# Turning the output gates of four memory heads together and ahead of the softmax, in a two-layer encoder on one core

## The chip, the core and the metric

The kernel runs on one core of a Trainium2 chip. That core has five engines, each with its own instruction stream that is worked off in order: TensorE (PE: matmuls, with PEld for the loading of their stationary operand), VectorE (DVE), ScalarE (ACT), GpSimd (POOL) and SyncE (SP), which here does almost nothing but start DMA transfers. The transfers themselves run on 16 DMA engines. The metric is the device time of one execution in microseconds (us); a clock of 1.00 in the tables is TensorE at full speed.

## The reference

Input: 256 tokens of 2048 numbers, float32, and 256 memory tokens. Two layers, each of this form:

```python
h = rmsnorm(x, norm_g[l]);  proj = h @ w_in[l]
a_x, a_b, a_c, a_g, d_q, d_k, d_v, d_g, m_q, m_g = split(proj)
y_a = short_gated_conv(a_x, a_b, a_c, ...) * silu(a_g)          # 6 groups of 128 columns
y_d = rmsnorm(diff_attention(q, k, v, ...)) * (1 - lam) * silu(d_g)   # 6 heads of 128
mk, mv = from the memory tokens and w_mem_kv[l]
mq = rmsnorm(m_q per head)
y_m = (softmax(mq @ mk.T * 128 ** -0.5) @ mv) * silu(m_g)       # 4 heads of 128
x = x + concat(y_a, y_d, y_m) @ w_out[l]
```

The change concerns the line of `y_m`: `softmax(...)` is a 256x256 matrix for each of four heads, and `silu(m_g)` holds, for each head, 256 tokens by 128 columns.

## The kernel before

**The main stream.** All weights come from HBM in loads of two k-tiles (`load_w`, L289, on SP's queue: 512 KB as one DMA, or two of 256 KB, four buffers). ACT rounds a load to `hi` (L292), DVE computes `lo`, the raw weights less `hi` (L293), and PE multiplies both with the split activations (L303: 12 matmuls of 128x512 for each load, three products for each of two token tiles and two k-tiles). `hi` and `lo` have four buffers too. In the text, weight loads are counted over the whole program in the order in which SP starts them. A projection block of 512 columns takes eight loads.

**The side work.** Between the blocks' matmuls stand pieces of attention, written as Python generators. A task is put into a list with a due number of chunks (`later`), and at each chunk of the stream the due generators run on to their next `yield`. So a `yield 4` sets how many chunks later the next step stands in the instruction streams. Counters `held` keep the tasks within the buffers: two softmax tiles `e`, two sheets `sh`, two tiles `yn`. Pins (`keep_in_program_order`) and a scheduler set the final order on each engine.

**Turning a matrix.** The attention needs matrices with rows and columns exchanged. DVE transposes blocks of 32x32 within a tile, and `carry` (L423 to L434) exchanges the blocks by way of DRAM: four DMAs write the sheet out (L430), two chunks later four read it back (L434). All eight are on SP's queue, where the weight loads stand too, and a read waits on SP for the landing of the writes.

**A memory pair** (`mem_pair`, two of the four heads; two pairs for each layer). `mem_scores` splits the turned queries `mqT` into two parts (ACT L604, L606; DVE L605, L607), multiplies with the keys (PE L613 to L615, tile `s`), takes exponentials `e` and gives back `e` and `r`, the reciprocal of the row sums times the half token scale `st[:, HR]`. The pair then transposes `e` into a sheet `sh`, multiplies the gate rows `mga` of each head by `r` into `yn` (L651, two for each head), transposes `yn` (L654), and carries first `sh` and then `yn` through DRAM. Last, PE computes `po` (L686): values times turned softmax weights, with channels on the partitions, and DVE multiplies `po` by the turned `yn` into the final `y`. A pair holds one of the two `yn` buffers, which the differential heads' pairs (`pair`) use as well, from before its transposes to its end.

The gate rows `mga` come from the projection block of `m_g`: `silu2` (L436 to L441) writes them, one 128x512 half for each token tile.

Of the kernel before, what the change touches and what calls it, by code (L numbers as in the profile page):

```python
# [10 lines left out]
F32 = mybir.dt.float32  # L11
# [3 lines left out]
ALU = mybir.AluOpType  # L15
# [3 lines left out]
P = 128  # L19
D_MODEL = 2048  # L20
SEQ = 256
DEPTH = 2
NT = SEQ // P
KT = D_MODEL // P
W_MEM = 512
# [3 lines left out]
DH = W_DIFF // P  # L29
# [3 lines left out]
NB = 512  # L33
# [3 lines left out]
B = 32  # L37
NA = P // B
# [10 lines left out]
def encoder(ctx: ExitStack, tc: tile.TileContext, x, mem, norm_g, w_in, conv_w, conv_b,  # L49
            dq_g, dk_g, lq1, lk1, lq2, lk2, head_g, mem_norm_g, w_mem_kv, mq_g, mk_g, w_out, out):  # L50
    nc = tc.nc
# [9 lines left out]
    keep = pool("keep", 1)  # L61
    tmp = pool("tmp", 2)
# [8 lines left out]
    def nm(s):  # L71
        uid[0] += 1
        return f"{s}_{uid[0]}"
# [134 lines left out]
    side, tasks = deque(), []  # L208
# [3 lines left out]
    def later(g, n):  # L212
        due[id(g)] = chunk[0] + n
        return g
# [181 lines left out]
    def sheet(home, tag, n=NB // P):  # L396
        return home.tile([P, NA, n, NT, B], F32, tag=tag, name=nm("sh"))
# [27 lines left out]
    def carry(sheet, to):  # L425


        d = dram.tile([NA, B, NA, sheet.shape[-1]], F32, name=nm("d"))
        for a in range(NA):
            tc.keep_in_program_order(nc.sync.dma_start(d[:, :, a].rearrange("b c r -> c b r"), sheet[a * B:(a + 1) * B]))  # L430
        yield 2
        of = d.rearrange("b c a (n i) -> (b c) a n i", i=B)
        for a in range(NA):
            tc.keep_in_program_order(nc.sync.dma_start(to[:, :, a], of[:, a]))  # L434

    def silu2(dst, src, st, t):  # L436

        n = src.shape[-1]
        th = tmp.tile([P, NB], F32, tag="nat", name=nm("th"), bufs=3)
        nc.scalar.activation(th[:, 0:n], src, AF.Tanh, scale=col(st, HR, t))  # L440
        nc.vector.scalar_tensor_tensor(dst, th[:, 0:n], 1.0, src, ALU.add, ALU.mult)  # L441

    def strips(v):
        return v.rearrange("p (b c) -> p b c", c=B)
# [63 lines left out]
    held = {"e": 0, "sh": 0, "yn": 0}  # L508
# [89 lines left out]
    def mem_scores(l, h, st):  # L598
        while l not in queries:
            yield 1  # L600
        qT, parts = queries[l]
        q, k, g = qT[:, h], mkT[l][:, h], mgain[:, l:l + 1]
        qh, ql, kh, kl = (parts[:, j] for j in (2 * (h % 2), 2 * (h % 2) + 1, 4, 5))
        pin(nc.scalar.copy(qh, q))  # L604
        pin(nc.vector.tensor_tensor(ql, q, qh.bitcast(F32), ALU.subtract))  # L605
        pin(nc.scalar.activation(kh, k, AF.Copy, scale=g))  # L606
        pin(nc.vector.scalar_tensor_tensor(kl, k, g, kh.bitcast(F32), ALU.mult, ALU.subtract))  # L607
        yield 1
        sc = P ** -0.5
        s = ps_s.tile([P, NT, SEQ], F32, tag="s", name=nm("s"))  # L610
        for i in range(NT):
            at = slice(i * P, (i + 1) * P)
            nc.tensor.matmul(s[:, i, :], qh[:, at], kh, start=True, stop=False)  # L613
            nc.tensor.matmul(s[:, i, :], qh[:, at], kl, start=False, stop=False)
            nc.tensor.matmul(s[:, i, :], ql[:, at], kh, start=False, stop=True)  # L615
        mx = small.tile([P, NT], F32, tag="mmx", name=nm("mmx"))
        nc.vector.tensor_reduce(mx, s, AX.X, ALU.max)
        nc.vector.tensor_scalar(mx, mx, -sc, None, ALU.mult)
        sm = small.tile([P, NT], F32, tag="msm", name=nm("msm"))
        e = tmp.tile([P, NT, SEQ], F32, tag="e", name=nm("me"))  # L620
        for i in range(NT):
            nc.scalar.activation(e[:, i], s[:, i], AF.Exp, bias=mx[:, i:i + 1], scale=sc, accum_out=sm[:, i:i + 1])
        r = small.tile([P, NT], F32, tag="mr", name=nm("mr"), bufs=6)
        nc.vector.reciprocal(r, sm)
        nc.vector.tensor_tensor(r, r, st[:, HR], ALU.mult)
        return e, r

    spare, yTs = {}, {}

    def mem_pair(l, n, a, st):  # L630
        heads = (2 * n, 2 * n + 1)
        es = []
        for h in heads:
            while held["e"] == 2:
                yield 1
            held["e"] += 1
            es.append((yield from mem_scores(l, h, st)))
            yield 2
        yield 4
        while held["sh"] == 2 or held["yn"] == 2:  # L640
            yield 1
        held["sh"] += 1
        held["yn"] += 1
        sh = tmp.tile([P, NA, 2, NT * NT, B], F32, tag="sh", name=nm("sh"))
        yn = tmp.tile([P, NA, 2, NT, B], F32, tag="yn", name=nm("yn"))
        for i, (e, r) in enumerate(es):
            tc.keep_in_program_order(nc.vector.transpose(
                sh[:, :, i], e.rearrange("p t (k b c) -> p b (t k) c", k=NT, b=NA)))
            held["e"] -= 1
            for t in range(NT):  # L650
                nc.vector.tensor_scalar(yn[:, :, i, t], strips(a[:, t, heads[i] * P:(heads[i] + 1) * P]),  # L651
                                        r[:, t:t + 1], None, ALU.mult)
            yield 1
        tc.keep_in_program_order(nc.vector.transpose(yn, yn))  # L654
        yield 4
        eT = sh.rearrange("p b h n c -> p (b h n c)")
        yT_ = yn.rearrange("p b h t c -> p (b h t c)")
        yield from carry(sh.rearrange("p b h n c -> p b (h n c)"), eT.rearrange("p (n a i) -> p n a i", a=NA, i=B))
        yield from carry(yn.rearrange("p b h t c -> p b (h t c)"), yT_.rearrange("p (n a i) -> p n a i", a=NA, i=B))
        if n == 0:  # L660
            spare[l] = [keep.tile([P, 3, NB], F32R, tag=tag, name=nm(tag)) for tag in ("v", "ga")]
        hi, lo = spare[l]

        def split(j, src):
            tc.keep_in_program_order(nc.scalar.copy(hi[:, j], src))
            tc.keep_in_program_order(nc.vector.tensor_tensor(lo[:, j], src, hi[:, j].bitcast(F32), ALU.subtract))

        yield 1
        for k in range(NT):
            c = slice(k * SEQ, (k + 1) * SEQ)  # L670
            src = mv[l][:, k, n * SEQ:(n + 1) * SEQ]
            tc.keep_in_program_order(nc.scalar.copy(hi[:, 0, c], src))
            tc.keep_in_program_order(nc.vector.tensor_tensor(lo[:, 0, c], src, hi[:, 0, c].bitcast(F32), ALU.subtract))
        split(1, eT[:, 0:NB])
        yield 1
        split(2, eT[:, NB:2 * NB])
        held["sh"] -= 1
        yield 1
        for i, h in enumerate(heads):
            po = ps_t.tile([P, SEQ], F32, tag="t", name=nm("po"))  # L680
            at = 0
            for k in range(NT):
                vh, vl = (t[:, 0, k * SEQ + i * P:k * SEQ + (i + 1) * P] for t in (hi, lo))
                eh, el = (t[:, 1 + i].rearrange("p (t k q) -> p t k q", t=NT, k=NT)[:, :, k] for t in (hi, lo))
                for left, right in ((vh, eh), (vh, el), (vl, eh)):
                    nc.tensor.matmul(po, left, right, start=at == 0, stop=at == 3 * NT - 1)  # L686
                    at += 1
            y = yT_[:, i * SEQ:(i + 1) * SEQ]
            nc.vector.tensor_tensor(y, po, y, ALU.mult)
            yield 2  # L690
            assert all((l, d) in scored for d in range(DH))
            split_T(yTs[l], CG + DH + h, y, None, pin=True)
        held["yn"] -= 1

    def rows_T(src, k, n):

# [272 lines left out]
    while s < DEPTH * KT:  # L969
        l, k = divmod(s, KT)  # L970
# [24 lines left out]
    for l in range(DEPTH):  # L995
        st = stats_of(ssx, "st")
# [12 lines left out]
        def begin_pair(n, p):  # L1009
            tasks.append(later(p, max(1, start + PAIR_EVERY * n - chunk[0])))  # L1010
# [4 lines left out]
        for b in order:  # L1015
            if b in begun:
                acc = x_block([(C_D + b * NB, NB)], ALLK[-QT:], acc=begun[b])
            else:
                acc = x_block([(C_D + b * NB, NB)], ready=m.ready if l == 0 and b == order[0] else None)
# [21 lines left out]
                        silu2(ga[:, t, 256:768], acc[t], st, t)  # L1041

        mqT = keep.tile([P, MH, SEQ], F32, tag="mqT", name=nm("mqT"))
        mga = keep.tile([P, NT, W_MEM], F32, tag="mga", name=nm("mga"))
        acc = x_block([(C_M, NB)])

        def turn_mq(nat):
# [4 lines left out]
        tasks.append(later(turn_mq(normed(acc, P, st, sheets("bgx"))), 8))  # L1052
        acc = x_block([(C_M + W_MEM, NB)])
        for t in range(NT):
            silu2(mga[:, t, :], acc[t], st, t)
        for n in range(MH // 2):
            begin_pair(DH // 2 + n, mem_pair(l, n, mga, st))


        bg = sheet(keep, "bgx", CG)  # L1060
# [54 lines left out]
        acc = x_block([(C_B, NB)])  # L1115
        scaled(both_rows(bg, 0, 4), acc, HR2)
        acc = x_block([(C_B + NB, 256), (C_G + NB, 256)])
        scaled(both_rows(bg, 4, 6), [a[:, 0:256] for a in acc], HR2)
        gate(NB, 256, [a[:, 256:512] for a in acc])
        acc = x_block([(C_G, NB)])  # L1120
        gate(0, NB, acc)
        tasks.append(later(turn_bg(list(range(CG))), 6))
        acc = x_block([(C_X, NB)])
        ux = sheet(keep, "bgx", CG)
        scaled(both_rows(ux, 0, 4), acc, R2)
        acc = x_block([(C_C, NB)])
        times(both_rows(ux, 0, 4), acc)
        tasks.append(later(conv([0, 1, 2, 3], ux), 6))
        acc = x_block([(C_X + NB, 256), (C_C + NB, 256)])
# [10 lines left out]
        for b in range(4):  # L1140
# [3 lines left out]
            for t in range(NT):  # L1144
                n = 256 if final else NB
# [43 lines left out]
```

## Time and profile before

| what | value |
|---|---|
| median of 3 runs | 928.33 us (927.62 to 928.81) |
| the profiled execution's own time | 926.78 us |
| its span (first to last instruction) | 925.0 us |
| mean granted TensorE clock | 0.997 |
| PE busy | 917.3 us (99%) |
| DVE, ACT, POOL busy | 680.4, 505.7, 36.6 us |

The span is what the views of the trace cover; 1.8 us of the profiled execution lie around it. Engines run beside each other, so busy times are not to be added. PE is busy in 99% of the span, so a change shows in the time through PE: by instructions it gets or loses, by time in which it waits, or by its clock.

### The profile page before, as it was taken

Reading aid. Unit: us, or ns where it says so; the run is one execution under the profiler, and the core shown is the slowest. Engines: PE = TensorE matmul, PEld = TensorE weight load, DVE = VectorE, ACT = ScalarE, POOL = GpSimd, SP = SyncE. Lnnn points to the kernel's source line nnn. Section 1 sums busy time; section 2 is a strip of 40 time slices with the busy share of each in tenths; the row PEclk is TensorE's granted clock in tenths of the full one; section 3 lists DMA queues with packets and bytes.
Section 4 is the critical chain, followed back from the end, with each engine's and each line's share of the span. In section 5 each row is a group of like instructions: output and inputs, shape, how many; then the busy total and the mean of one; then the engine's idle time right before and its main releaser. Section 6 shows DMA issues by size and latency. Waiting matters only on the chain.

```text
span 925.0 us, 12351 instructions
## 1 busy us (share of the span) xinstructions
PE 917.3 (99%) x4177; PEld 761.3 (82%) x4177; DVE 680.4 (74%) x1217; ACT 505.7 (55%) x781; POOL 36.6 (4%) x66
## 2 busy tenths in 40 slices
PE   9999999999999999989999999999999999999998
PEld 6888888888888888878888888888888888888887
DVE  5579978857898797567666757887898788478652
ACT  6667645675545565345555544568555555356431
POOL 2334010000000000000000000000000000000000
PEclk9999999999999999999999999999999999999999
DMA  8889877876669979998587767886888869998662
GB/s 287 290 243 264 271 245 221 269 210 195 178 223 242 223 239 231 235 300 239 200 280 243 237 187 221 238 237 187 235 233 215 252 200 253 234 276 252 218 217 78
DMA packets 247023, 215.11 MB, mean 233 GB/s; under 512 B 132130, under 2 KB 172912, under 8 KB 246960
## 3 DMA queue, kind: packets, MB, share of 16 engines
q1 hardware_dynamic: 242080, 208.71, 77.1%
q0 software_dynamic: 3680, 4.56, 2.1%
q10 hardware_dynamic: 1200, 1.07, 0.4%
q8 instruction: 32, 0.52, 0.2%
q14 instruction: 31, 0.25, 0.1%
HBM read 193.26 MB, written 20.97 MB: 232 GB/s over the span
## 4 chain that ended last, share of the span: by engine, by line
PE 94%; SPq 3%; DMA 1%; DVE 1%; issue 0%; ACT 0%; ACTq 0%; DVEq 0%
PE acc L303 89%; DMA raw<-in_w_in_dram 1%; SPq L434 1%; PE po L451 1%; SPq L430 1%; PE s L559 1%; PE s L558 1%; DVE lo L293 0%; PE acc L870 0%; PE po L686 0%; PE pt L700 0%; SPq L289 0%; PE warm L124 0%; ACT hi L292 0%; PE s L615 0%
## 5 line engine op out<-in xcount | busy, mean ns | idle before, releaser
L303 PE MATMUL acc<-hi,xT 128*128 128x512 f32 x1792 | 560.0, 391 | 1.9 <-ACT hi L292 1.9
L292 ACT CAST hi<-raw 128x1024 fp32r<-128x1024 f32 x280 | 294.1, 1052 | 328.3 <-PE acc L303 230.5
L293 DVE TENSOR_TENSOR lo<-raw,hi 128x1024 fp32r<-128x1024 f32 x280 | 341.4, 1221 | 170.2 <-ACT hi L292 167.4
L303 PEld LDWEIGHTS acc<-hi,xT 128*128 128x128 f32 x1792 | 337.2, 188 | 71.3 <-ACT hi L292 2.4
L303 PE MATMUL acc<-lo,xT 128*128 128x512 f32 x896 | 349.8, 390 | 0.8 <-DVE lo L293 0.8
L303 PEld LDWEIGHTS acc<-lo,xT 128*128 128x128 f32 x896 | 168.7, 188 | 35.1 <-DVE lo L293 1.1
L303 PE MATMUL acc<-hi,yT 128*128 128x512 f32 x512 | 157.2, 388 | 0.0
L303 PEld LDWEIGHTS acc<-hi,yT 128*128 128x128 f32 x512 | 96.0, 188 | 19.8
L303 PE MATMUL acc<-lo,yT 128*128 128x512 f32 (+1 forms) x256 | 99.3, 388 | 0.0
L303 PE MATMUL acc<-hi,memT 128*128 128x512 f32 x248 | 78.2, 393 | 0.0
L303 PEld LDWEIGHTS acc<-lo,yT 128*128 128x128 f32 x256 | 48.1, 188 | 9.9
L303 PEld LDWEIGHTS acc<-hi,memT 128*128 128x128 f32 x248 | 46.1, 188 | 9.3
L853 DVE SCALAR_TENSOR_TENSOR lo<-raw,cva,hi 128x1024 fp32r<-128x1024 f32 (+1 forms) x34 | 41.0, 1217 | 15.5 <-ACT hi L852 15.3
L303 PE MATMUL acc<-lo,memT 128*128 128x512 f32 x124 | 48.0, 391 | 0.0
L852 ACT ACTIVATE hi<-raw,cva 128x1024 fp32r<-128x1024 f32 (+1 forms) x34 | 36.4, 1099 | 12.0 <-DMA raw<-in_w_mem_kv_dram 11.8
L303 PEld LDWEIGHTS acc<-lo,memT 128*128 128x128 f32 x124 | 23.3, 188 | 5.5 <-DVE lo L853 0.7
L569 ACT ACTIVATE e<-e,mx 128x256 f32<-128x256 f32 x48 | 23.8, 498 | 1.4 <-DVE mx L565 1.3
L717 POOL DMA_DIRECT2D xt<-in_x_dram x32 | 21.5, 678 | 19.0 <-DVE rsy L187 13.2
L563 DVE SCALAR_TENSOR_TENSOR e<-dist,s 128x512 f32<-128x512 f32 x24 | 15.7, 679 | 2.2 <-PE s L559 1.7
L413 DVE STREAM_TRANSPOSE sh<-sh 128x1024 f32<-128x1024 f32 (+2 forms) x14 | 17.3, 1237 | 0.0
L262 ACT ACTIVATE xT<-xf,gx 128x256 fp32r<-128x256 f32 x32 | 14.4, 501 | 4.8 <-DVE xf L723 4.0
L723 DVE STREAM_TRANSPOSE xf<-xt 128x1024 f32<-128x1024 f32 x8 | 16.1, 2012 | 0.0
(183 smaller groups left out, 622.0 us busy)
## 6 DMA issues: line engine op xcount, KB each, us to landing
raw<-in_w_in_dram SPq DMA_DIRECT2D x192, 512.0 KB, 4.4
raw<-in_w_out_dram SPq DMA_DIRECT2D x64, 512.0 KB, 4.3
raw<-in_w_in_dram SPq DMA_DIRECT2D x64, 256.0 KB, 4.5
raw<-in_w_mem_kv_dram SPq DMA_DIRECT2D x30, 512.0 KB, 6.3
d<-sh SPq DMA_DIRECT2D x80, 128.0 KB, 3.8
sh<-d SPq DMA_DIRECT2D x64, 128.0 KB, 4.3
d<-yn SPq DMA_DIRECT2D x40, 64.0 KB, 3.0
yn<-d SPq DMA_DIRECT2D x40, 64.0 KB, 4.6
```

The source lines that it names most:

```text
L262: both = (nc.scalar.activation(hi, src, AF.Copy, scale=gain), nc.vector.scalar_tensor_tensor(lo, src, gain, hi.bitcast(F32), ALU.mult, ALU ...
L292: nc.scalar.copy(hi, raw)
L293: nc.vector.tensor_tensor(lo_, raw, hi.bitcast(F32), ALU.subtract)
L303: i = nc.tensor.matmul(acc, left, right, start=start, stop=stop)
L413: tc.keep_in_program_order(nc.vector.transpose(src, src))
L430: tc.keep_in_program_order(nc.sync.dma_start(d[:, :, a].rearrange("b c r -> c b r"), sheet[a * B:(a + 1) * B]))
L563: nc.vector.scalar_tensor_tensor(e[:, c], dist, -slopes[h], s[c], ALU.mult, ALU.add)
L569: nc.scalar.activation(e[:, c, i], e[:, c, i], AF.Exp, bias=mx[:, c, i:i + 1], accum_out=sm[:, c, i:i + 1])
L717: tc.keep_in_program_order(nc.gpsimd.dma_start(st[:, n], src[n * B:(n + 1) * B].rearrange("p (b r) -> b p r", b=NA)))
L723: tc.keep_in_program_order(nc.vector.transpose(whole.rearrange("p j (n i) -> p j n i", i=B), st.rearrange("p n (c j) -> p j n c", j=QT)))
L852: both = (nc.scalar.activation(hi[:, j], raw[:, j], AF.Copy, scale=g), nc.vector.scalar_tensor_tensor(lo[:, j], raw[:, j], g, hi[:, j].bit ...
L853: nc.vector.scalar_tensor_tensor(lo[:, j], raw[:, j], g, hi[:, j].bitcast(F32), ALU.mult, ALU.subtract))
```

## The change

`mem_scores` now multiplies `e` by `r` itself (two instructions of 128x256 for each head) and gives back `e` alone. The gates are no longer multiplied by `r`. Their tile `mga` becomes a sheet: right behind the `m_g` block each token tile's half goes into a passing tile `a` and is transposed (L1051, 128x512) into `mga`, and one `carry` task, due 11 chunks later, turns all four heads' gates through DRAM, in place. `mem_pair` loses the tile `yn`, its multiplications, its transpose, its `carry` and its wait for a free `yn` buffer; the end multiplies `po` by the turned gates of the head (`gates[l][:, h]`).

```diff
         r = small.tile([P, NT], F32, tag="mr", name=nm("mr"), bufs=6)
         nc.vector.reciprocal(r, sm)
         nc.vector.tensor_tensor(r, r, st[:, HR], ALU.mult)
-        return e, r
+        for i in range(NT):
+            nc.vector.tensor_scalar(e[:, i], e[:, i], r[:, i:i + 1], None, ALU.mult)
+        return e
...
-    def mem_pair(l, n, a, st):
+    def mem_pair(l, n, st):
...
-        while held["sh"] == 2 or held["yn"] == 2:
+        while held["sh"] == 2:
             yield 1
         held["sh"] += 1
-        held["yn"] += 1
         sh = tmp.tile([P, NA, 2, NT * NT, B], F32, tag="sh", name=nm("sh"))
-        yn = tmp.tile([P, NA, 2, NT, B], F32, tag="yn", name=nm("yn"))
-        for i, (e, r) in enumerate(es):
+        for i, e in enumerate(es):
             tc.keep_in_program_order(nc.vector.transpose(
                 sh[:, :, i], e.rearrange("p t (k b c) -> p b (t k) c", k=NT, b=NA)))
             held["e"] -= 1
-            for t in range(NT):
-                nc.vector.tensor_scalar(yn[:, :, i, t], strips(a[:, t, heads[i] * P:(heads[i] + 1) * P]),
-                                        r[:, t:t + 1], None, ALU.mult)
             yield 1
-        tc.keep_in_program_order(nc.vector.transpose(yn, yn))
         yield 4
...
-        yield from carry(yn.rearrange("p b h t c -> p b (h t c)"), yT_.rearrange("p (n a i) -> p n a i", a=NA, i=B))
...
-            y = yT_[:, i * SEQ:(i + 1) * SEQ]
+            y = gates[l][:, h]
             nc.vector.tensor_tensor(y, po, y, ALU.mult)
...
-        held["yn"] -= 1
...
-        mga = keep.tile([P, NT, W_MEM], F32, tag="mga", name=nm("mga"))
+        mga = sheet(keep, "mga")
...
         for t in range(NT):
-            silu2(mga[:, t, :], acc[t], st, t)
+            a = tmp.tile([P, NB], F32, tag="nat", name=nm("a"), bufs=3)
+            silu2(a, acc[t], st, t)
+            tc.keep_in_program_order(nc.vector.transpose(mga[:, :, :, t], a.rearrange("p (j b c) -> p b j c", b=NA, c=B)))
+        gates[l] = mga.rearrange("p b j t i -> p (b j t i)").rearrange("p (j r) -> p j r", r=SEQ)
+        tasks.append(later(carry(mga.rearrange("p b j t i -> p b (j t i)"),
+                                 gates[l].rearrange("p j (t a i) -> p (j t) a i", t=NT, a=NA)), 11))
         for n in range(MH // 2):
-            begin_pair(DH // 2 + n, mem_pair(l, n, mga, st))
+            begin_pair(DH // 2 + n, mem_pair(l, n, st))
```

**Where it moves instructions.** The rows below are SP's stream in program order (line, operation, target and source tile with the instance's number, shape, repeats). `raw` is a weight load, `d` a carry's scratch in DRAM; a `d<-` row is a carry's writes, a `<-d` row its reads.

The first place is layer 0, the late weight load of the profile, which is raw_3792 (load 136). Before, between load 133 (raw_3718) and the loads behind it:

```order
L289 DMA raw_3718<-in_w_in_dram 128x2x512
L430 DMA d_3736<-sh_3583 32x4x256 x4
L434 DMA bgT_3557<-d_3685 128x12x32 x4
L289 DMA raw_3747<-in_w_in_dram 128x2x512
L289 DMA raw_3765<-in_w_in_dram 128x2x512
L434 DMA sh_3583<-d_3736 128x8x32 x4
L430 DMA d_3787<-yn_3584 32x4x128 x4
L289 DMA raw_3792<-in_w_in_dram 128x2x512
L289 DMA raw_3814<-in_w_in_dram 128x2x256 x2
```

Now, from the second memory pair's carry to load 136, which is raw_3803 here:

```order
L430 DMA d_3661<-sh_3513 32x4x256 x4
L289 DMA raw_3666<-in_w_in_dram 128x2x512
L289 DMA raw_3684<-in_w_in_dram 128x2x512
L430 DMA d_3702<-sh_2679 32x4x384 x4
L434 DMA sh_3513<-d_3661 128x8x32 x4
L289 DMA raw_3711<-in_w_in_dram 128x2x512
L289 DMA raw_3735<-in_w_in_dram 128x2x512
L434 DMA bgT_3588<-d_3702 128x12x32 x4
L289 DMA raw_3759<-in_w_in_dram 128x2x512
L289 DMA raw_3785<-in_w_in_dram 128x2x512
L289 DMA raw_3803<-in_w_in_dram 128x2x512
```

The second pair's sheet goes out and comes back before load 132 (raw_3711) instead of around load 135, the writes and reads of its `yn` are gone, and behind `bgT`'s reads come three loads with nothing between them. (`bgT` is the convolution's gates, turned by a carry of its own.)

The second place is some ten loads earlier, the first memory pair in layer 0. Before, from load 123 (raw_3468) on:

```order
L289 DMA raw_3468<-in_w_in_dram 128x2x512
L430 DMA d_3458<-yn_3048 32x4x128 x4
L430 DMA d_3463<-sh_3286 32x4x256 x4
L289 DMA raw_3486<-in_w_in_dram 128x2x512
L434 DMA yn_3048<-d_3458 128x4x32 x4
L434 DMA sh_3286<-d_3463 128x8x32 x4
L430 DMA d_3514<-yn_3287 32x4x128 x4
L289 DMA raw_3519<-in_w_in_dram 128x2x512
```

Now, from the first memory pair's carry (d_3407) to load 125 (raw_3550):

```order
L430 DMA d_3407<-sh_3241 32x4x256 x4
L289 DMA raw_3412<-in_w_in_dram 128x2x512
L289 DMA raw_3442<-in_w_in_dram 128x2x512
L434 DMA sh_3241<-d_3407 128x8x32 x4
L289 DMA raw_3466<-in_w_in_dram 128x2x512
L430 DMA d_3484<-yn_3061 32x4x128 x4
L289 DMA raw_3495<-in_w_in_dram 128x2x512
L289 DMA raw_3517<-in_w_in_dram 128x2x512
L434 DMA yn_3061<-d_3484 128x4x32 x4
L289 DMA raw_3550<-in_w_in_dram 128x2x512
```

The pair's `yn` (yn_3287) is gone, its sheet moved ahead by some four loads, and the differential pair's `yn` (yn_3048, now yn_3061) has loads between its writes and its reads. From load 124 up to load 136 SP has 36 transfers beside the loads before, and 20 now.

The third place is where the gates' own carry stands, again in layer 0. Before, from load 104 (raw_2894) on:

```order
L289 DMA raw_2894<-in_w_in_dram 128x2x512
L430 DMA d_2880<-yn_2419 32x4x128 x4
L434 DMA mqT_2160<-d_2839 128x8x32 x4
L289 DMA raw_2933<-in_w_in_dram 128x2x256 x2
L289 DMA raw_2963<-in_w_in_dram 128x2x256 x2
```

Now, in the same place, with the gates' sheet named sh_2161 and its scratch d_3013:

```order
L289 DMA raw_2898<-in_w_in_dram 128x2x512
L289 DMA raw_2939<-in_w_in_dram 128x2x256 x2
L289 DMA raw_2969<-in_w_in_dram 128x2x256 x2
L430 DMA d_2884<-yn_2419 32x4x128 x4
L434 DMA mqT_2160<-d_2843 128x8x32 x4
L289 DMA raw_2994<-in_w_in_dram 128x2x256 x2
L430 DMA d_3013<-sh_2161 32x4x256 x4
L289 DMA raw_3042<-in_w_in_dram 128x2x256 x2
L289 DMA raw_3093<-in_w_in_dram 128x2x256 x2
L434 DMA sh_2161<-d_3013 128x8x32 x4
L289 DMA raw_3116<-in_w_in_dram 128x2x256 x2
```

The reads of the turned queries `mqT` stand behind two more loads (105 and 106), and the gates' eight transfers stand behind loads 107 and 109. In layer 1 their four writes stand behind load 251, the 16 transfers that stood behind load 251 before stand behind load 252, and the gates' four reads behind load 253. On PE the four heads' scores and products (L613 to L615, L686) stand three to seven loads earlier than before, except the first two heads' scores.

More of the change, by code (lines that the diff above doesn't have):

```diff
@@ L625, in mem_scores @@
         nc.vector.tensor_tensor(r, r, st[:, HR], ALU.mult)
-        return e, r
-    spare, yTs = {}, {}
-    def mem_pair(l, n, a, st):
+        for i in range(NT):
+            nc.vector.tensor_scalar(e[:, i], e[:, i], r[:, i:i + 1], None, ALU.mult)
+        return e
+    spare, yTs, gates = {}, {}, {}
+    def mem_pair(l, n, st):
         heads = (2 * n, 2 * n + 1)
@@ L649, in mem_pair @@
             held["e"] -= 1
-            for t in range(NT):
-                nc.vector.tensor_scalar(yn[:, :, i, t], strips(a[:, t, heads[i] * P:(heads[i] + 1) * P]),
-                                        r[:, t:t + 1], None, ALU.mult)
             yield 1
-        tc.keep_in_program_order(nc.vector.transpose(yn, yn))
         yield 4
         eT = sh.rearrange("p b h n c -> p (b h n c)")
-        yT_ = yn.rearrange("p b h t c -> p (b h t c)")
         yield from carry(sh.rearrange("p b h n c -> p b (h n c)"), eT.rearrange("p (n a i) -> p n a i", a=NA, i=B))
-        yield from carry(yn.rearrange("p b h t c -> p b (h t c)"), yT_.rearrange("p (n a i) -> p n a i", a=NA, i=B))
+        assert l in gates
         if n == 0:
```

## The prediction, made before the changed kernel ran

> **What bounds the kernel now.** The page's first two lines say how much there is to win without taking work from PE.
>
> ```profile
> span 925.0 us, 12351 instructions
> PE 917.3 (99%) x4177; PEld 761.3 (82%) x4177; DVE 680.4 (74%) x1217; ACT 505.7 (55%) x781; POOL 36.6 (4%) x66
> ```
>
> PE is idle for 7.7 us. I next read what PE waited for, in total:
>
> ```profile
> PE acc L303 <- ACT hi L292: 1.9, 1, 1.9
> PE acc L303 <- DVE lo L293: 0.8, 1, 0.8
> ```
>
> Both waits occur once; the rest of the idle time is start and end. The chain of waits gives their place. From 349 to 391 it runs along SP's starts and some loads, elsewhere in mid-kernel along PE; that piece ends with:
>
> ```profile
> 390.85 4.32 DMA raw<-in_w_in_dram
> 395.27 1.05 ACT hi L292
> 396.35 1.24 DVE lo L293
> ```
>
> A load started at 390.85, landed 4.32 later, was rounded, and only then had PE its `hi`. The busy time by stretches (columns: length, then PE, PEld, DVE, ACT, POOL; then granted clock, DMA share, GB/s) shows what follows it:
>
> ```profile
> 390.00:400.00 10.00, 7.31 (x27) 5.45 (x26) 3.77 (x5) 3.68 (x6) 0.00 (x0) 0.90 1.01 252
> 400.00:410.00 10.00, 10.00 (x43) 8.15 (x42) 8.72 (x12) 5.33 (x7) 0.00 (x0) 0.93 1.02 333
> 430.00:440.00 10.00, 10.00 (x46) 8.29 (x45) 9.46 (x19) 6.66 (x11) 0.00 (x0) 1.00 0.84 256
> 398.00:400.00 2.00, 2.00 (x6) 1.61 (x5) 1.49 (x2) 1.59 (x4) 0.00 (x0) 0.50 0.89 214
> 400.00:402.00 2.00, 2.00 (x7) 1.55 (x7) 1.99 (x4) 1.43 (x3) 0.00 (x0) 0.66 0.99 295
> ```
>
> Behind the wait the granted clock is 0.50, then 0.66, and PE is "busy" at half speed. The stall's price two ways: idle 1.9 + 0.8 = 2.7, plus 2.00 x 0.50 + 2.00 x 0.34 = 1.7 of lost clock, makes 4.4 us. Or by matmuls: 27 + 43 in 20 us where an undisturbed stretch has 46 in 10, so 22 missing at 10/46 = 0.217 us each, 4.8 us. I take the middle, 4.6.
>
> Why was that load late? SP's own rows (start, length, transfers), all the carries' rows since 345.58 and three of the loads':
>
> ```profile
> 345.58 0.39 SPq L289 DMA_DIRECT2D raw<-in_w_in_dram  x1
> 346.08 2.14 SPq L434 DMA_DIRECT2D yn<-d  x4
> 348.38 3.44 SPq L434 DMA_DIRECT2D sh<-d  x4
> 351.87 3.82 SPq L430 DMA_DIRECT2D d<-yn  x4
> 355.78 1.43 SPq L289 DMA_DIRECT2D raw<-in_w_in_dram  x3
> 357.39 2.91 SPq L434 DMA_DIRECT2D yn<-d  x4
> ...
> 367.77 2.65 SPq L430 DMA_DIRECT2D d<-sh  x4
> ...
> 373.12 2.42 SPq L430 DMA_DIRECT2D d<-sh  x4
> 375.65 5.25 SPq L434 DMA_DIRECT2D bgT<-d  x4
> ...
> 383.79 4.67 SPq L434 DMA_DIRECT2D sh<-d  x4
> 388.51 2.25 SPq L430 DMA_DIRECT2D d<-yn  x4
> 390.85 2.46 SPq L289 DMA_DIRECT2D raw<-in_w_in_dram  x5
> ```
>
> SP is one queue in order. From 345.58 (load 124) to 390.85 (load 136) it spends 2.14 + 3.44 + 3.82 + 2.91 + 2.65 + 2.42 + 5.25 + 4.67 + 2.25 = 29.6 us on 36 carry transfers, 0.82 each, and the loads stand behind them. Four buffers hold only three loads ahead of the one in use, and a load lasts PE 2.74 us (24 matmuls take 5.47 in the chain's row quoted further below, and a load has 12). Two clumps, 12 transfers from 346.08 and 8 from 383.79, spend that lead.
>
> **The change part by part.** SP in this stretch: 16 of the 36 transfers go (yn_3287's eight, yn_3584's four writes, and the first pair's sheet reads, which now stand earlier), 20 stay. At 0.82 each SP is 16 x 0.82 = 13 us earlier at load 136, against a stall of 2.7 and a full lead of three loads, 8.2. So the load comes as early as its buffer allows, and the stall goes whole: -4.6. What is late next there would be load 134 behind `bgT`'s four reads (5.25), but the second sheet's reads no longer follow them, and the loads after it come one behind another (355.78: three starts in 1.43).
>
> The work that comes instead, on DVE, has these neighbours:
>
> ```profile
> L651 DVE TENSOR_SCALAR yn<-mga,mr 128x128 f32<-128x128 f32 x16 | 3.5, 279 | 0.0
> L654 DVE STREAM_TRANSPOSE yn<-yn 128x512 f32<-128x512 f32 x4 | 2.8, 701 | 0.0
> L576 DVE SCALAR_TENSOR_TENSOR e<-e,cf 128x256 f32<-128x256 f32 x24 | 10.6, 480 | 0.2
> ```
>
> Removed over the program: 16 x 0.279 + 4 x 0.701 = 7.3 us. Added: four transposes of the same shape, 2.8, and 16 multiplications of 128x256, a form the trace lacks: between 0.279 (half the elements) and 0.480 (as many elements, two tensors read). I take 0.480, its nearest by size: 7.7. Net +3.2 us (range 0 to +3.2) over two layers. DVE is busy 680.4 of 925.0, so 245 us of it are free and this costs nothing; without that cover, 3.2 at most. Each head's chain from exponentials to transposed sheet gets 2 x 0.48 = 1 us longer. The pair waits at least four chunks behind its second head's scores for its transposes, so it lies inside; who waits next is SP, with the sheet's writes. The final multiplication keeps its form: 0. PE gets and loses no instruction: 0.
>
> The gates' carry adds eight transfers a layer (of 128 KB, against 16 of 64 KB removed, so the bytes are the same). Two places get them.
>
> Layer 0, loads 104 to 110: the rows there before, and the first score's:
>
> ```profile
> 283.79 2.56 SPq L289 DMA_DIRECT2D raw<-in_w_in_dram  x2
> ...
> 288.50 4.05 SPq L434 DMA_DIRECT2D mqT<-d  x4
> ```
> ```profile
> 295.96 0.48 DVE L607 SCALAR_TENSOR_TENSOR parts<-mkT,mgain,parts 128x256 fp32r<-128x256 f32 x1
> ```
> ```profile
> L613 PE MATMUL s<-parts x2: 282/282/283, 303.6 to 304.0; 128*128 128x256 f32 x2
> ```
>
> `mqT`'s reads are put behind two more loads: 2.56 later by the loads' own row, at most 2 x 2.74 = 5.5 where their buffers set the pace. The parts, ready at 296.4 now, would be ready at 299.0 to 301.9, and the scores that need them are at 303.6: 1.7 to 4.6 us to spare. I count 0. While ACT waits for `mqT`, the `hi` of load 106 is queued behind it, and PE needs that only after the scores.
>
> Layer 1, loads 251 to 254: 16 transfers stand there now, and 24 after the change.
>
> ```profile
> 705.58 1.90 SPq L430 DMA_DIRECT2D d<-yn  x4
> 707.58 1.82 SPq L430 DMA_DIRECT2D d<-sh  x4
> 709.81 2.06 SPq L434 DMA_DIRECT2D yn<-d  x4
> 712.04 2.56 SPq L434 DMA_DIRECT2D sh<-d  x4
> 714.70 10.55 SPq L289 DMA_DIRECT2D raw<-in_w_in_dram  x11
> ```
> ```profile
> 727.28 5.47 PE acc L303 x24
> ```
>
> The 16 took 705.58 to 714.70, 0.57 each. PE reaches load 253 in the middle of the last row, at 730.0. After the change 20 transfers and load 252 (two DMAs, 1.1 at the same pace) stand ahead of it: 705.6 + 20 x 0.57 + 1.1 = 718.1, landed 4.4 later (the page's row below), rounded 1.05 after that: 723.6, 6.4 us to spare. I count 0, and the bounds of the unknown pace are in the last rival. The sum is -4.6: 926.78 becomes 922.2 for the profiled execution. The median of the runs lies 1.55 above that execution, so against 928.33 I forecast 923.7, with 922.6 to 924.8 as this case's own range (stall 4.4 to 4.8, the three runs' spread of 1.2).
>
> **A rule against the trace.** The rows above put the clock of 0.50 right behind two waits of 1.9 and 0.8. The Trainium skill, page "TensorE: Matmul & The Clock Gate", section "Why this matters for your kernels", says that gaps up to about 3 us between matmul bursts do no harm and that one idle window (about 3.4 us in its Part 1) halves the clock. By that rule these waits would not have slowed PE, and the trace here shows that they did; it is the first rival below.
>
> **The rivals.** *The slow clock is not the stall's.* Had it another cause (a transition that comes anyway, at about 398), only the 2.7 of idle go: 924.1, on the median 925.6. For it: no other wait of this length is there to compare. Against it: the clock is down in the slice behind the wait and nowhere else in mid-kernel (0.90 and 0.93 in these two stretches, 1.00 in 430:440).
>
> *The queue is not the cause, the DMA engines are.* The bytes stay the same, and the DMA share in 390:400 is 1.01. Then the stall moves but is not shorter: 926.8, on the median 928.3. Against it: this load took 4.32 from start to landing, and the page has
>
> ```profile
> raw<-in_w_in_dram SPq DMA_DIRECT2D x192, 512.0 KB, 4.4
> ```
>
> as the median of all, so it was not slow once started; it was started late. On the other hand a start itself can be held up for long, as two neighbours in the chain show:
>
> ```profile
> 384.26 0.57 SPq L434
> 384.89 2.75 SPq L434
> ```
>
> If busy engines hold it, fewer starts do not help. The Trainium skill, page "DMA: Bandwidth & Descriptors", section "Issuing engines are not separate DMA queues", speaks for this rival: all transfers run on the same 16 engines, and a queue saves only the time to start them.
>
> *A new stall at layer 0's first scores.* If `mqT` comes later than the bounds above, by another load's 2.74, PE waits 1 to 2.7 us at 303.6 and then runs at half clock for 1.7: 2.7 to 4.4 given back, on the median 926.4 to 928.1, say 927.3. For it: the margin's lower end is 1.7. Against it: it takes the slowest pace and one load more.
>
> *Slower: layer 1's 24 transfers starve load 253.* This decides once a transfer's average start costs more than (730.0 - 1.05 - 4.4 - 705.6 - 1.1) / 20 = 0.89 us; 0.82 is the average of layer 0's stretch, `bgT`'s were 1.31. At 1.31 load 253 starts at 705.6 + 26.2 + 1.1 = 732.9, its `hi` is ready at 738.4, PE waits 8.4 and loses 1.7 by the clock: +10.1, less 4.6, makes 932.3, on the median 933.8. Against it: the 16 that stand there now had 0.57, and four of the 24 stand a load earlier than the others.
>
> **How the numbers follow.** The stall's removal 0.69; the clock rival 0.04 (also faster); the DMA engines 0.06 and the first scores 0.07 (both about unchanged); layer 1's clump 0.14 (slower). A measurement of this kernel can tell about 0.2%, 1.9 us, from no change: faster 0.73, same 0.13, slower 0.14. The range from 922.3 to 928.1 leaves out the last rival and little else.
>
> **What would show it.** Right: no `acc` wait on `hi` at 380 to 410, about 46 matmuls in each 10 us there with clock 1.00, PE idle near 5, SP starting load 136 some 10 us before its use. Wrong: a clock below 1.00 in another stretch, a wait of L613 on `parts` near 304, or a load in the chain near 730. If SP's rows between 345 and 390 still sum to 30 us though they hold 20 transfers, the second rival holds.

## The result, and the profile after

The changed kernel took 924.55 us (median of 7, 924.14 to 926.18) beside 928.2 of the kernel before (median of 7, 927.62 to 929.97). The ratio is 0.9963, with a 95% interval of 0.9951 to 0.9974: 3.4 us faster, by the interval 2.4 to 4.5. The profiled execution took 924.14 us against 926.78. The page's first lines and the waits of PE that are over 0.5 us, after:

```profile
span 922.4 us, 12335 instructions
PE 915.3 (99%) x4177; PEld 759.7 (82%) x4177; DVE 677.4 (73%) x1217; ACT 503.9 (55%) x781; POOL 36.5 (4%) x66
```
```profile
PE warm L124 <- DVE zeros L119: 1.2, 1, 1.2
PE po L451 <- DMA sh<-d: 1.2, 1, 1.2
PE acc L303 <- DVE lo L847: 0.8, 2, 0.6
```

The waits of 1.9 and 0.8 near 395 are gone, and so is the slow clock behind them. In their place in the list stands a new wait of 1.2, of a differential pair's product `po` (L451). (The wait on L847 is in the first 13 us.) The two stretches around the old stall, with the columns as before:

```profile
390.00:400.00 10.00, 10.00 (x49) 8.32 (x48) 7.59 (x8) 5.58 (x6) 0.00 (x0) 1.00 1.01 335
400.00:410.00 10.00, 10.00 (x48) 8.38 (x47) 6.76 (x9) 4.44 (x5) 0.00 (x0) 1.00 0.68 215
```

97 matmuls stand where 70 stood before. The span's balance: the stall's -4.4 (idle and clock), the new wait's +1.2, and +0.6 by which this execution's first loads came later, make -2.6, which is 922.4 - 925.0. Without the start, which differs from one execution to the next, -3.2 are left beside the 3.4 measured.

SP's rows from load 124's time to load 136, after:

```profile
352.10 2.02 SPq L434 DMA_DIRECT2D yn<-d  x4
...
363.76 1.94 SPq L430 DMA_DIRECT2D d<-sh  x4
...
368.71 2.67 SPq L430 DMA_DIRECT2D d<-sh  x4
371.49 3.76 SPq L434 DMA_DIRECT2D sh<-d  x4
...
376.67 6.81 SPq L434 DMA_DIRECT2D bgT<-d  x4
383.58 2.81 SPq L289 DMA_DIRECT2D raw<-in_w_in_dram  x3
```

The 20 transfers took 17.2 us, 0.86 each. The last row holds loads 134 to 136, so load 136 started at about 386, not 390.85. It came 5 us earlier, not the 13 that the sum had.

### The profile page after: what moved, and what is told of

Read it like the earlier page. It is cut to its first block, busy times and chain, and to the rows that moved or that the text cites. A ratio compares the mean times of both kernels' runs of the same rounds, so it can differ in the third digit from the quotient of the medians.

```text
span 922.4 us, 12335 instructions
## 1 busy us (share of the span) xinstructions
PE 915.3 (99%) x4177; PEld 759.7 (82%) x4177; DVE 677.4 (73%) x1217; ACT 503.9 (55%) x781; POOL 36.5 (4%) x66
## 4 chain that ended last, share of the span: by engine, by line
PE 94%; DMA 3%; SPq 1%; DVE 1%; ACT 1%; issue 0%; ACTq 0%
PE acc L303 90%; DMA raw<-in_w_in_dram 2%; PE po L451 1%; DMA raw<-in_w_mem_kv_dram 1%; PE s L559 1%; PE po L681 1%; PE s L558 1%; SPq L434 1%; DVE lo L293 1%; DMA mqT<-d 0%; DMA sh<-d 0%; PE pt L694 0%; ACT hi L292 0%; SPq L827 0%; PE s L614 0%
## 5 line engine op out<-in xcount | busy, mean ns | idle before, releaser
L847 DVE SCALAR_TENSOR_TENSOR lo<-raw,cva,hi 128x1024 fp32r<-128x1024 f32 (+1 forms) x34 | 41.0, 1218 | 15.2 <-ACT hi L846 15.0
```

Of the source, the lines that this page charges most:

```text
L847: nc.vector.scalar_tensor_tensor(lo[:, j], raw[:, j], g, hi[:, j].bitcast(F32), ALU.mult, ALU.subtract))
```

## The experiments

Each ratio is to the kernel before on the same chip, in brackets its 95% interval. The kernel before had medians of 928.7, 929.2 and 929.5 us in the three sets of runs (925.7 to 933.7 for single executions), so ratios are compared, and medians within a set. The first set holds the next four runs.

**The memory pairs' yn on another queue.** In the kernel before, where `carry` also gets the queue as an argument (`...` marks what is left out of a line):

```diff
-        yield from carry(yn.rearrange(...), yT_.rearrange(...))
+        yield from carry(yn.rearrange(...), yT_.rearrange(...), q=nc.gpsimd)
```

> The kernel before with one edit: the carry of each memory pair's yn (8 transfers of 64 KB) stands on GpSimd's queue instead of SyncE's. Bytes, pairs and everything else stay. If the order of starts on SyncE's queue made the load late (my theory): SyncE loses 12 of its 36 carry transfers between loads 124 and 136 (0.82 us each, 10 us), no wait of the accumulation on hi near 395, no half clock there, and the time is 4.4 us below before, near 923.8. If the 16 DMA engines made it late (rival): the bytes are still there, the wait of 1.9 + 0.8 stays within 1 us, and the time is near 928.2. Memory pairs' gates may come late instead, since their reads start on another engine: a wait of the final product would show on VectorE, not on PE.

Measured: 927.45 us, 0.9983 (0.9969 to 0.9998), 1.6 us faster and not 4.4. In the profiled execution the waits near 390 to 397 are smaller (0.5 and 0.8), and the clock stays at 1.00, but SP's starts did not become quicker:

```profile
375.18 5.94 SPq L434 DMA_DIRECT2D bgT<-d  x4
381.22 2.72 SPq L289 DMA_DIRECT2D raw<-in_w_in_dram  x2
384.03 6.21 SPq L434 DMA_DIRECT2D sh<-d  x4
```

The sheet's four reads took 4.67 before and 6.21 here, with fewer transfers on SP's queue and `yn`'s reads running from GpSimd's at 380.56. So a start's length is no fixed price. That busy DMA engines hold the starts up, as the second rival has it, would fit; the DMA share was over 1.0 in both stretches (1.11 before, 1.02 here), so these rows alone do not show it. The profiled execution (925.01) was the fastest of the twelve. In all twelve the mean clock was 0.999 or 1.000, so the slow clock is gone in each; what made the others up to 4 us slower, no trace tells.

**No yn carry at all.** In the kernel before:

```diff
-        yield from carry(yn.rearrange(...), yT_.rearrange(...))
+        yield 2
```

> The kernel before without the carry of the memory pairs' yn at all (16 transfers a layer gone, the pair keeps its buffers and waits; it leaves out the exchange of the gates' blocks by way of DRAM, so the memory heads are gated by blocks that stand in the wrong places). My theory: the stall near 395 goes, as in the changed kernel, and the new 1.2 us wait of po on a sheet near 322 is not there, since nothing is added to layer 0's clump: 928.2 - 4.4 = 923.8. Rival (it is the earlier start of the memory pairs that takes the stall away, not the transfers): the stall stays, near 928.

Measured: 923.16 us, 0.9934 (0.9916 to 0.9953). The stall as such is gone without the pairs being any earlier; what is left of it is a wait of 0.2 and one of 0.8, at 394 to 396:

```profile
PE acc L303 <- DVE lo L293: 0.8, 1, 0.8
...
PE acc L303 <- ACT hi L292: 0.2, 1, 0.2
```

Here too the last starts ahead of load 136 stayed long (`bgT`'s four 5.99, the sheet's four 6.04). To take the transfers from SP's queue gave 1.6 us, and to take them away as a whole 4.3 more (923.16 against 927.45). The prediction counted starts on SP alone, so something besides them weighs more. That it is the bytes is the nearest reading but not shown, because the first run also starts the transfers from another engine and at other times.

**The gates' carry on another queue.** In the changed kernel, again with the queue as an argument of `carry`:

```diff
-                                 gates[l].rearrange(...)), 11))
+                                 gates[l].rearrange(...), q=nc.gpsimd), 11))
```

> The changed kernel with the gates' carry on GpSimd's queue. If the gates' eight transfers on SyncE's queue are what delays the differential pair's sheet near 317 to 323 (theory): its reads start some 6.9 us earlier (the gates' 1.95 + 4.94), the 1.2 us wait of po goes, and the time is 1.2 below the changed kernel, 923.3. If the DMA engines' load delays them (rival): the same bytes move at the same time, the wait stays near 1.2 and the time near 924.5.

Measured: 925.16 us, 0.9954 (0.9936 to 0.9972). The wait of `po` fell from 1.2 to 0.3, so the gates' transfers do stand behind it. Yet the sheet's reads started only 2 us earlier (314.21 for 316.17, not 6.9), as the order puts them behind load 112 still, and waits of 0.4 and 0.8 at load 134 took the place. No gain over the changed kernel.

**The gates' carry later.** In the changed kernel:

```diff
-                                 gates[l].rearrange(...)), 11))
+                                 gates[l].rearrange(...)), 20))
```

> The changed kernel with the gates' carry due 20 chunks later instead of 11: in layer 0 its writes then stand behind load 116 and its reads behind load 118, past the clump; in layer 1 behind loads 260 and 262. Theory: the sheet's reads stand right behind the writes again as before the change, po waits for nothing, 923.3 (1.2 below the changed kernel), and the smallest lead of a load in layer 1's clump (2.9 at load 254) goes up to 5 or more. Rival: the clump was late for another reason (the turned queries' reads behind two more loads), and the wait stays: 924.5.

Measured: 923.56 us, 0.9941 (0.9919 to 0.9963). The wait of `po` is gone: the sheet's reads stand at 308.87 again, where they had stood before (308.51). The time is not told apart from the changed kernel's 0.9963 by the intervals. The one wait of PE over 0.5 that is left in mid-kernel is 0.8 on `lo`, at load 134 near 390.

The second set follows.

**A carry of 64 KB pieces put back.** In the changed kernel's pair, behind the sheet's carry:

```diff
+        flat = gates[l][:, 2 * n:2 * n + 2].rearrange("p h r -> p (h r)")
+        yield from carry(flat.rearrange("p (b r) -> p b r", b=NA), flat.rearrange("p (n a i) -> p n a i", a=NA, i=B))
```

> The changed kernel with a second carry of 64 KB pieces (4 writes, 4 reads) behind each memory pair's sheet, where yn's carry stood before; it carries half of the gates once more, so the gates' blocks end in the wrong places. The pairs stay early. If the last clump ahead of loads 134 to 136 is what decides (my theory after the first runs: earlier transfers don't matter, since the lead is full again by load 130), four writes behind load 131 and four reads ahead of load 134 are back, about 6 us of SyncE's time against load 134's lead of 1.2: PE waits 3 to 5 us for hi near 391, perhaps with half clock behind it, and the time is 928 to 931. If the earlier start of the pairs was enough by itself (rival): no such wait, 924.6.

Measured: 941.12 us, 1.013 (1.0104 to 1.0156), worse than expected, because both layers have the stall:

```profile
PE acc L303 <- ACT hi L292: 7.7, 3, 3.1
PE acc L303 <- DVE lo L293: 2.1, 3, 0.8
```

Layer 1's is a single wait of 2.7 that ends at 812.7, and the clock behind it reads:

```profile
805.00:810.00 5.00, 5.00 (x23) 3.81 (x21) 0.00 (x0) 0.00 (x0) 0.00 (x0) 1.00 1.10 157
810.00:815.00 5.00, 2.27 (x6) 1.53 (x6) 2.27 (x4) 3.35 (x6) 0.00 (x0) 0.71 0.98 355
815.00:820.00 5.00, 5.00 (x18) 4.02 (x18) 4.29 (x6) 3.24 (x4) 0.00 (x0) 0.61 0.78 222
```

That is 5.00 x 0.29 + 5.00 x 0.39 = 3.4 us of lost clock for 2.7 of idle (some 0.3 of it still within the wait, by stretches of 1 us). The early pairs do not protect from the stall; the traffic ahead of loads 134 to 136 decides. And the slow clock follows the wait to a place where it never was before, which speaks against the rival that it had another cause. But it does not follow every such wait. In layer 0 of this execution PE waited 1.9 and, 0.5 us later, 0.8 (up to 390.4), as in the kernel before, and then 3.1 (up to 399.0):

```profile
385.00:390.00 5.00, 2.71 (x11) 1.69 (x9) 0.91 (x1) 1.72 (x3) 0.00 (x0) 1.00 1.13 233
390.00:395.00 5.00, 4.63 (x20) 3.85 (x21) 1.88 (x3) 0.68 (x1) 0.00 (x0) 1.00 0.95 139
395.00:400.00 5.00, 1.92 (x6) 0.85 (x5) 1.05 (x1) 2.13 (x5) 0.00 (x0) 0.90 0.94 337
400.00:405.00 5.00, 5.00 (x21) 4.16 (x21) 5.00 (x8) 3.97 (x6) 0.00 (x0) 0.75 0.93 279
```

Behind the first two waits the clock stayed at 1.00; only behind the third did it fall.

**The pairs held back.** In the changed kernel the pair waits for a free `yn` place again, and holds it:

```diff
-        while held["sh"] == 2:
+        while held["sh"] == 2 or held["yn"] == 2:
             yield 1
         held["sh"] += 1
+        held["yn"] += 1
...
             split_T(yTs[l], CG + DH + h, y, None, pin=True)
+        held["yn"] -= 1
```

> The changed kernel in which a memory pair still waits for one of the two yn places and holds it (the counter alone, no tile), so that both pairs stand where they stood before: the second sheet's reads are behind load 135 again, ahead of load 136, as before, but without yn's transfers. If removing the transfers is enough: 924.5, no wait but the known 1.2 near 322. If the earlier pairs take a part (my theory now, since without the transfers alone a wait of 0.9 stayed in the kernel before): waits of 0.5 to 1.5 in all near 392 to 396 and no half clock, 925.2 to 926. If the earlier pairs are all of it: the whole stall of 4.4 is back, 928.9.

Measured: 931.01 us, 1.0020 (1.0001 to 1.0039): all three were missed. The waits:

```profile
PE acc L303 <- DVE lo L293: 2.7, 4, 0.8
PE po L451 <- DMA sh<-d: 1.2, 1, 1.2
...
PE acc L303 <- ACT hi L292: 0.9, 2, 0.7
```

Some are at places that nobody had named. The chain that ends in the one near 339 is

```profile
325.57 6.25 DMA yn<-d
...
331.84 0.52 ACT yT L262
...
332.39 0.48 DVE yT L263
```

A differential pair's `yn`, read back behind the crowd at loads 110 to 113, landed 6.25 after its start; ACT and DVE had its split in front of the next weight loads' `hi` and `lo`, and DVE worked off the rest of its side work one after another until `lo` was late. The last run below tells how much of this is the gates' carry.

**bgT's carry later, in the kernel before.**

```diff
-        tasks.append(later(turn_bg(list(range(CG))), 6))
+        tasks.append(later(turn_bg(list(range(CG))), 12))
```

> The kernel before with one number changed: the carry of the convolution's gates (bgT) is due 12 chunks after its block instead of 6, so its four writes and four reads of 192 KB move from loads 131 and 133 to loads 137 and 139, out of the clump ahead of loads 134 to 136. Nothing is taken away. If the stall is a matter of which transfers stand together ahead of load 136 (theory): it goes as a whole, 928.3 - 4.4 = 923.9, unless a smaller one appears near load 140. If it is a matter of the number or the bytes of the transfers (rival): it moves some loads on and stays, 928.

Measured: 927.23 us, 0.9982 (0.9966 to 0.9998), 1.7 us faster. Load 136 landed early enough this time (it started at 385.43). Its `hi` was late all the same:

```profile
393.47 1.27 ACT L1109 ACTIVATE sh<-acc,st 128x512 f32<-128x512 f32 x2 [8.29 <-DMA d<-sh]
394.63 1.99 ACT L292 CAST hi<-raw 128x1024 fp32r<-128x1024 f32 x2
```

ACT waited 8.29 us for `bgT`'s writes (started from 386.91 to 390.15), because the next block's sheet uses the buffer that these read, and load 136's `hi` was queued behind that on ACT. So the theory failed in part: the crowd can be moved, but the move made another wait.

**Both carries later, in the changed kernel.** The gates' due 20 instead of 11, `bgT`'s 12 instead of 6.

> The changed kernel with both carries moved to free places: the gates' due 20 chunks later instead of 11, bgT's 12 instead of 6. With the gates' move alone a wait of 0.8 was left at load 134. Theory: that one goes too, no wait in mid-kernel is left, 922.8 to 923.2, which is what PE's instructions, start and end make. Rival: the last wait isn't from the clump, 923.6 as with the gates' move alone.

Measured: 922.29 us, 0.9935 (0.9913 to 0.9956), better than expected. PE's waits in the whole program:

```profile
PE warm L124 <- DVE zeros L119: 1.2, 1, 1.2
PE acc L303 <- DVE lo L847: 0.2, 1, 0.2
PE acc L864 <- ACT hi L846: 0.2, 1, 0.2
```

All three lie in the first 10 us. The span was 920.0.

The third set has the last four runs, with the changed kernel among them.

**The changed kernel again.**

> The changed kernel once more, beside the two below on the same chip. Its first comparison gave 0.9963 of the time before (0.9951 to 0.9974); expected again: 0.995 to 0.997, a wait of po on a sheet near 322 of about 1.2, no other in mid-kernel.

Measured: 925.07 us (12 executions, 923.88 to 928.99), 0.9958 (0.9945 to 0.9970), so the gain is confirmed. The execution that was profiled took 928.99, the longest of the twelve, and it shows one way in which single ones differ. Of the 4.9 us between it and the first profiled execution, 3.3 lie in the span (925.7 against 922.4), the rest outside it. Its waits, its clock and SP's starts:

```profile
PE acc L303 <- ACT hi L292: 1.3, 1, 1.3
...
PE po L451 <- DMA sh<-d: 1.2, 1, 1.2
PE acc L303 <- DVE lo L293: 0.8, 1, 0.8
```
```profile
390.00:395.00 5.00, 2.92 (x10) 1.85 (x9) 3.13 (x3) 3.14 (x3) 0.00 (x0) 0.87 1.05 392
395.00:400.00 5.00, 5.00 (x22) 4.15 (x21) 3.37 (x5) 2.50 (x3) 0.00 (x0) 0.79 1.09 334
```
```profile
371.49 5.14 SPq L434 DMA_DIRECT2D sh<-d  x4
376.73 1.05 SPq L289 DMA_DIRECT2D raw<-in_w_in_dram  x2
377.87 6.76 SPq L434 DMA_DIRECT2D bgT<-d  x4
384.74 3.42 SPq L289 DMA_DIRECT2D raw<-in_w_in_dram  x3
```

The same four reads of the sheet took 3.76 in the first profile and 5.14 here, and load 134 started 1.2 later (384.74 for 383.58); its `hi` began at 390.53 for 388.78. That was enough for waits of 1.3 and 0.8 and for a clock loss of 5.00 x 0.13 + 5.00 x 0.21 = 1.7. The change moved the stall to the edge at load 134; it did not put it out of reach.

**Both carries later, again.**

> The changed kernel with the gates' carry due 20 chunks later and bgT's 12, once more beside the changed kernel itself. If its gain is the 1.2 of the po wait and what was left at load 134: 1.2 to 2.5 us below the changed kernel on this chip, no wait in mid-kernel.

Measured: 922.24 us (921.20 to 923.71), 0.9925 (0.9911 to 0.9939), 2.8 us below the changed kernel in the same set, a little more than the 1.2 to 2.5 expected; no wait in mid-kernel. This version beats both kernels.

**The scaling twice.** In the changed kernel:

```diff
             nc.vector.tensor_scalar(e[:, i], e[:, i], r[:, i:i + 1], None, ALU.mult)
+            nc.vector.tensor_scalar(e[:, i], e[:, i], 1.0, None, ALU.mult)
```

> The changed kernel with each scaling of the softmax weights done twice (the second by 1.0), 16 more VectorE instructions of 128x256, 0.35 us each, 5.6 in all. If VectorE's added work is hidden, as I counted it: the same time as the changed kernel within 0.5 us, 5.6 more busy time on VectorE. If the chain from exponentials to the turned sheet lies on the path: up to 4 x 0.7 us more in each layer for the four heads, 927 to 930.

Measured: 927.34 us (924.92 to 929.41), 0.9982 (0.9967 to 0.9996), 2.3 above the changed kernel in its set (the two intervals just touch). The first multiplication in the changed kernel, and the added one here:

```profile
L627 DVE TENSOR_SCALAR me<-me,mr x16: 342/348/354, 309.0 to 759.4; 128x256 f32<-128x256 f32 x16
```
```profile
L628 DVE TENSOR_SCALAR me<-me x16: 283/289/290, 309.8 to 764.2; 128x256 f32<-128x256 f32 x16
```

The added ones took 0.29 us each, 4.6 in all and not 5.6, and they are not hidden as a whole. In the profiled execution the wait of `po` is 1.7 where it was 1.2, and waits of 0.3 and 0.8 stand at load 134; which of the added instructions delays which transfer wasn't separated.

**The pairs held back and the gates' carry later.** The kernel with the counter, and 20 for 11.

> The kernel with the pairs held back to their old places (931.0 where 925.2 to 926 was expected), and with the gates' carry due 20 chunks later, out of the clump at loads 107 to 112. If that clump's lateness is a part of the surprise: the waits near 321 (1.2) and 339 (0.6) go, those near 369 and 392 to 401 stay, 928 to 929. If the late pairs alone make it: 931.

Measured: 924.97 us (924.73 to 925.77), 0.9955 (0.9939 to 0.9971). The one number moves the held kernel from 1.0020 to 0.9955, 6 us. The waits near 321, 339 and 369 are gone, and 0.7 + 0.8 at 395 to 396 stay. So the gates' carry in the crowd at loads 107 to 112 made most of the surprise, and with the carry out of the crowd, held pairs cost little: 0.9955 beside 0.9941 for early pairs, which the intervals do not tell apart.

## Why the prediction came out as it did

**The time.** Forecast 923.7, measured 924.55; against the same kernel before, -4.6 was forecast and -3.4 measured. The sign, the place and the size of the main term were right. That the time fell into the range of 922.6 to 924.8 owes something to luck. From one profiled execution to the other the change was -2.6 (926.78 to 924.14) where -4.6 was forecast. The forecast then added 1.55, by which the median lay above the profiled execution before; after the change it lies only 0.41 above. With 1.55 the measured 924.14 would have become 925.7, outside the range.

**The stall goes whole, -4.6.** Right in the first profile (4.4 by idle and clock), not in every execution: in the one of 928.99 waits of 1.3 and 0.8 and the slow clock came back.

**SP is 13 us earlier at load 136.** This step was wrong in size. The stretch's carry starts did fall from 29.6 to 17.2 us, but load 136 started only 5 us sooner. The step added up savings over the whole stretch, though SP waits for free buffers in the middle of it, and what is saved ahead of such a wait is lost there. SP's own waits from 360 to 376 in the kernel before tell it:

```profile
SPq L289 <- DVE lo L293: 5.7, 3, 2.4
SPq L289 <- DVE mr L624: 1.7, 1, 1.7
```

The lead was full again by then, so the first of the "two clumps" was no cause. Load 131 had to wait for its buffer in both kernels and started at 367.35 before and at 368.27 after: of all that was saved ahead of it, nothing was left. Behind it the carry starts fell from 2.65 + 2.42 + 5.25 + 4.67 + 2.25 = 17.2 to 2.67 + 3.76 + 6.81 = 13.2 us, because the second sheet's writes stand further ahead and `yn`'s are gone. That is 4 of the 5 us.

**What is late next: load 134.** Named rightly, and dismissed too quickly. It is the load that PE waits for in the execution of 928.99, and in several of the variants.

**Layer 0's added transfers, counted 0.** This is the term that failed: +1.2. The scores, for which the margin was worked out, did not wait; their last part was ready at 300.5, inside the 299.0 to 301.9 that was given. But the reads of the differential pair's sheet, which come further back in the same crowd, were not followed to PE. In the kernel before and after:

```profile
304.38 1.76 SPq L430 DMA_DIRECT2D d<-sh  x4
306.24 2.10 SPq L434 DMA_DIRECT2D yn<-d  x4
308.51 2.42 SPq L434 DMA_DIRECT2D sh<-d  x4
```
```profile
298.02 1.95 SPq L430 DMA_DIRECT2D d<-sh  x4
...
302.84 4.94 SPq L434 DMA_DIRECT2D sh<-d  x4
...
309.08 1.92 SPq L430 DMA_DIRECT2D d<-sh  x4
...
316.17 4.51 SPq L434 DMA_DIRECT2D sh<-d  x4
```

The first two rows after are the gates' eight transfers, 6.9 us. The pair's reads moved by 7.7, and `po` waited 1.2 for them. The rival of a new stall in layer 0 thus came true in kind, one reader further on and at less than half its price.

**Layer 1's 24 transfers, counted 0.** Right. Load 253 started at 715.8, where 718.1 was forecast, and PE did not wait. The slower rival never came near its point: the 16 transfers just ahead of load 253 took 0.58 us each, and it needed 0.89.

**VectorE's work, counted 0.** The unknown multiplication took 0.349 us, between the bounds 0.279 and 0.480, so by the rows the net was about 1.4 more (4.9 + 2.8 added, 3.5 + 2.8 removed) and not 3.2. But "245 us free" was no proof of cover: 4.6 more cost about 2.3. Free time summed over a kernel doesn't lie where the late work is.

**The queue or the engines.** The prediction gave the engines 0.06. The runs put the truth between: to clear the queue alone gave 1.6 of the 6 us that removal gave, and the second sheet's four read starts took from 3.2 to 6.2 us in different runs. But their length does not follow the DMA share: 3.76 at 1.03 and 5.14 at 0.88 in two executions of the changed kernel, 6.21 at 1.02 with `yn` on GpSimd's queue, 5.50 at 0.70 with `bgT`'s carry later in the kernel before. So the engines' mean load does not explain it, and what does stays open. What the Trainium skill says in "DMA: Bandwidth & Descriptors", section "Issuing engines are not separate DMA queues", fits these rows where it has all transfers share the 16 engines; where it calls the time to start a transfer usually small beside the transfer itself, the rows differ (1.7 us a start for `bgT`'s four, in 6.81, beside 6.6 from start to landing).

**The clock.** The price of 1.7 us for the slow clock held again in the execution of 928.99, and behind the wait of 3.1 with the carry put back; behind the 2.7 there it was twice that. Which waits bring it stays open. Single waits of 1.2 and 1.7 left the clock at 1.00, a single one of 2.7 did not. Of two waits close together, 1.9 and 0.8 brought it in the kernel before, 1.3 and 0.8 in the execution of 928.99, but 1.9 and 0.8 with the carry put back did not. And of the kernel before's 63 executions in the three sets, 15 have a mean clock of 1.000 (925.7 to 928.5 us). So the prediction's 4.4 is the price in its one profiled execution, not a fixed one. The Trainium skill, page "TensorE: Matmul & The Clock Gate", section "Why this matters for your kernels", advises no idle gaps over about 3 us; here the gap of 2.7 was already enough.

## What to carry to other kernels

Where a stream of loads shares an in-order queue with side transfers, a saving counted here only from the queue's last wait for a buffer to the late load; read that wait before adding up starts. A moved group of transfers is to be followed to every reader behind it on its queue, not to the first alone. The place of a carry was worth more than its queue: one due number, in the held kernel, moved 6 us.

## What the runs showed of the hardware that was not expected

The four starts of one sheet's reads on SP took from 3.2 to 6.2 us in different runs, 3.76 and 5.14 in two executions of one kernel, and their length does not follow the DMA share. In the profiled execution with the pairs' `yn` on GpSimd's queue, SP's remaining starts were not any quicker. A wait of 2.7 us cost about 3.1 us more by the clock behind it, more than itself, while waits of 1.9 and 0.8 us, 0.5 us apart, were followed by a clock of 0.50 in one execution and by one of 1.00 in another.
